# Splitting the tile of log-exponents in a gated-recurrence branch: one tile for keys, one for queries, one more buffer, and a small sum moved from GpSimd to VectorE

## The chip, the cores and the metric

The kernel runs on one core of one Trainium2 chip. The metric is the device time of one launch in microseconds (us). A difference is told against the median of the runs of the kernel before.

Engine names as the profile has them: PE is TensorE's matmul stream, PEld its weight loads, DVE VectorE, ACT ScalarE, POOL GpSimd, SP SyncE. A semaphore is what one engine waits on for another.

## The reference

A trunk of two layers over one sequence of 512 positions with 1024 channels. Each layer has three branches, and the change lies in the first:

```
z = RMSNorm(x) @ W_in            # columns are divided among the branches and gates
A: gated linear recurrence, 4 heads, 128 key and 128 value channels, forward and backward:
     log_f = logaddexp(log lb, log1p(-lb) + logsigmoid(zf));  key = (1 - lb) * sigmoid(-zf)
     state_t = exp(log_f_t) * state_(t-1) + key_t v_t ;  o_t = q_t . state_t   (chunks of 64)
     forward and backward o summed, RMS-normalized per head, times a SiLU gate
B: gated spatial mixing in chunks of 128
C: windowed attention, 8 query heads and 2 key heads of 64 channels, partial rotary, a sink logit
merge: each branch @ W_branch, times a sigmoid gate from xn, summed, @ W_out, added to x
x = x + (relu(RMSNorm(x) @ W_up) ** 2) @ W_down
```

After both layers comes a last RMSNorm. Everything is float32.

## The kernel before, in words

**Products.** Activations lie transposed (channels on the 128 partitions, the 512 positions along the free dimension). Every large product is done with three matmuls of 512 columns (`mm3`, L200 to L202), for which weights and activations are each split into a rounded high part and the low rest. A weight chunk of 512 KB is loaded on SP's queue, its high part is cast on ACT (L195, tile `wh`) and its low part subtracted on DVE (L196, tile `wl`). So all three engines serve the matmuls, beside what the branches themselves ask of ACT and DVE.

**Branch A, one head.** `a_ffb` does the head's two gate projections (matmuls into `f`, brought to the tile `z` on DVE in L693). `a_gates` turns them into a tile `ex` of four rows of 512 exponents: rows 0 and 2 hold the log keys of the forward and the backward direction, rows 1 and 3 the log forget gates that become the exponents of the queries. `a_head` then goes through seven levels L = 1, 2, 4 ... 64. Each level

- exponentiates a half of the query rows into `qt` (ACT, L552), multiplies it with the queries (DVE, L553), exponentiates a half of the key rows into `kt` (ACT, L555),
- does 16 small matmuls (`at`, L539) and puts the result where a mask says (DVE, L543; at L = 1 and L = 64 copies on ACT),
- and adds decays in place to the exponents: two sums of 512 columns on DVE (L580). Each of the two touches a key row and a query row.

At L = 1 there is also the diagonal: one exponential of both key rows (1024 columns, tile `key`, ACT L560), their sum into `dg` on POOL (L562), and 16 more matmuls. After the last level, for each direction the keys are decayed (`kd`, ACT L592), transposed on PE (`kT`, L595), copied (ACT, L597) and multiplied into states (`stp` on PE, L600; `st` on DVE), and the queries are decayed (`qd`, L609 and L610). Then `av` (PE, L623), its norm (`asq` on ACT, L628; `ms` on DVE, L260; `rs` on POOL, L262; `ao` on DVE, L631) and a transposition (`oT`, PE L635).

`qt`, `kt`, `dg`, `kd`, `qd`, `asq` and `ao` take turns in three buffers of the tag "a". `z`, `key` and a work tile of `a_gates` take turns in three buffers of another tag.

**Around it.** While the heads run, PE fills its time with the projections of the next heads (`f`), of branch C (`q`, with rotary on DVE in L867 to L870, L685 and L898), of the gates (`gz`) and of the merge (`yB`, `yC`, `yA`). Branch C's scores `sc` (L914, L915), transposed probabilities `pT` (L943) and products `po` (L948) are mixed in. Transfers of the merge (`mcd`, `th`, `mC`, `mB`) and of the residual (`xr`) are issued by POOL. A turn on PE (`mT`, L1023) sums them up after the last head.

**Who sets the order.** A scheduler with priorities builds the order of each engine's instructions from the program and from its own estimates of time; work of the merge has a low priority and fills. Each engine then runs its list strictly in that order, and waits at an instruction whose input or buffer isn't there. A change of the program therefore also changes which fill work stands between two steps of a head.

Of the kernel before, what the change touches and what calls it, by code (L numbers as in the profile page):

```python
# [10 lines left out]
ALU = mybir.AluOpType  # L11
# [48 lines left out]
def trunk(tc, xT, xt, ws, vec, fnb, bsb, snk, wst, rope, cmask, amask, ident, out):  # L60
# [4 lines left out]
    def pool(**kw):  # L65
# [21 lines left out]
    part = {}  # L87
    BANKS = {"m": 2, "a": 2, "c": 2, "s": 2}
    GROUPS = (("m", "m", "c", "c"), ("a", "a", "s", "s"))
    WR, WB, NZ, NCT, NSM, NQ = 2, 3, 3, 4, 3, 10  # L90

    def nm(s):
        ctr[0] += 1
        return f"{s}_{ctr[0]}"
# [13 lines left out]
        return part["br"].tile([P, 2, S], F32, tag="z2", bufs=NZ, name=nm(name))  # L108

    def SM(tag, w):  # L110
        return pad.tile([P, w], F32, tag="sm_" + tag, bufs=4 if tag == "lb" else NSM, name=nm(tag))

    def CT(name):
        return part["br"].tile([P, 3 * P], F32, tag="ct", bufs=NCT, name=nm(name))
# [384 lines left out]

    def a_gates(l, h, z2, lbs):  # L500

        ex = part["br"].tile([P, 4, S], F32, tag="ex", bufs=1, name=nm("ex"))
        lfo = [ex[:, 3], ex[:, 1]]
        e = Z2("ga")
        nc.scalar.activation(e, z2, AF.Abs)
        nc.scalar.activation(e, e, AF.Exp, scale=-1.0)
        nc.scalar.activation(e, e, AF.Ln, bias=onep_t[:, 0:1])
        if l == 0:
            for d in range(2):
                nc.vector.scalar_tensor_tensor(lfo[d], z2[:, d], 0.0, e[:, d], ALU.min, ALU.subtract)  # L510
                nc.vector.tensor_tensor(ex[:, 2 * d], lfo[d], z2[:, d], ALU.subtract)
        else:
            l1p, llb, dl = lbs
            u = e
            nc.vector.scalar_tensor_tensor(u, z2, 0.0, e, ALU.min, ALU.subtract)
            for d in range(2):
                c = slice(d * 4 + h, d * 4 + h + 1)
                nc.vector.scalar_tensor_tensor(ex[:, 2 * d], u[:, d], l1p[:, c], z2[:, d], ALU.add, ALU.subtract)
# [6 lines left out]
        return ex  # L525

    def a_head(l, h, ex, q, vt):
        H = P // 2
        at = part["br"].tile([P, 4, P], F32, tag="at", bufs=1, name=nm("at"))
        own = part["br"].tile([P, 4, H], F32, tag="own", bufs=1, name=nm("own"))  # L530

        def attn(kk, qq, other=False):

            pt = PT("a", "at")
            for st in range(4):
                for h_ in range(2):
                    k0 = st * P + h_ * H
                    q0 = st * P + (1 - h_ if other else h_) * H
                    nc.tensor.matmul(pt[h_ * H:(h_ + 1) * H, st * H:(st + 1) * H], kk[:, k0:k0 + H], qq[:, q0:q0 + H], start=True, stop=True, skip_group_check=True)  # L539
# [5 lines left out]
        X, R, Y, PP = 0, S, 2 * S, 3 * S  # L545
        for li, L in enumerate(LEVELS):
            nb = 256 // L
            shp = "p (b h i) -> p b h i"
            e_k = ap_of(ex, 0, [[2 * L, nb], [2 * S + L, 2], [1, L]])
            e_q = ap_of(ex, S, [[2 * L, nb], [2 * S + L, 2], [1, L]])  # L550
            qt = T("a", "qt")
            nc.scalar.activation(qt.rearrange(shp, b=nb, h=2), e_q, AF.Exp)  # L552
            nc.vector.tensor_tensor(qt, qt, q, ALU.mult)  # L553
            kt_ = T("a", "kt")
            nc.scalar.activation(kt_.rearrange(shp, b=nb, h=2), e_k, AF.Exp)  # L555
            if L == 1:
                pt = attn(kt_, qt)
                nc.scalar.copy(own, pt)
                key = Z2("key")
                nc.scalar.activation(key, ap_of(ex, 0, [[2 * S, 2], [1, S]]), AF.Exp)  # L560
                dg = T("a", "dg")
                nc.gpsimd.tensor_tensor(dg, key[:, 0], key[:, 1], ALU.add)  # L562
# [13 lines left out]
            d = [[2 * L, nb], [1, L]]  # L576
            z = [[2 * L, nb], [0, L]]
            for o_, ostep, i_, istep in ((X, PP + L - X, PP + 2 * L - 1, -L), (Y + L, R - Y - L, R, L)):
                o_ap = ap_of(ex, o_, [[ostep, 2]] + d)
                nc.vector.tensor_tensor(o_ap, o_ap, ap_of(ex, i_, [[istep, 2]] + z), ALU.add)  # L580

        W3 = 3 * P
        dec = SM("ms", 4)
        nc.scalar.activation(dec[:, 0:2], ap_of(ex, PP + 2 * P - 1, [[P, 2]]), AF.Exp)
        nc.scalar.activation(dec[:, 2:4], ap_of(ex, R + P, [[P, 2]]), AF.Exp)
        sts, qds = [], []
        for dr, (ko, qo) in enumerate(((0, P), (P, 0))):

            kd = T("a", "kd")[:, 0:W3]
            nc.scalar.activation(kd, ex[:, 2 * dr, ko:ko + W3], AF.Exp)  # L592
            pt = PT("a", "kT")
            for i in range(3):
                nc.tensor.transpose(pt[:, i * P:(i + 1) * P], kd[:, i * P:(i + 1) * P], id_t)  # L595
            kT = part["br"].tile([P, W3], F32, tag="kT", bufs=1, name=nm("kT"))
            nc.scalar.copy(kT, pt[:, 0:W3])  # L597
            ps_ = PT("a", "stp")
            for i in range(3):
                nc.tensor.matmul(ps_[:, i * P:(i + 1) * P], kT[:, i * P:(i + 1) * P], vt[ko // P + i][:, h * P:(h + 1) * P], start=True, stop=True)  # L600
# [8 lines left out]
            nc.scalar.activation(qd, ex[:, 3 - 2 * dr, qo:qo + W3], AF.Exp)  # L609
            nc.vector.tensor_tensor(qd, qd, q[:, qo:qo + W3], ALU.mult)  # L610
            sts.append(st_)
            qds.append(qd)

        po = PT("a", "av")
        for tt in range(4):
            c = slice(tt * P, (tt + 1) * P)
            parts = [(at[:, tt], vt[tt][:, h * P:(h + 1) * P])]
            if tt > 0:
                parts.append((qds[0][:, (tt - 1) * P:tt * P], sts[0][:, tt - 1]))
            if tt < 3:  # L620
                parts.append((qds[1][:, c], sts[1][:, tt]))
            for i, (w_, m_) in enumerate(parts):
                nc.tensor.matmul(po[:, c], w_, m_, start=i == 0, stop=i == len(parts) - 1)  # L623
        sq = T("a", "asq")
        ss = SM("ss", 4)
        for tt in range(4):
            c = slice(tt * P, (tt + 1) * P)
            nc.scalar.activation(sq[:, c], po[:, c], AF.Square, accum_out=ss[:, tt:tt + 1])  # L628
        rc = rstd_c(ss, P)
        o = T("a", "ao")  # L630
        nc.vector.tensor_tensor(o.rearrange("p (a b) -> p a b", a=4), po.rearrange("p (a b) -> p a b", a=4), ap_of(rc, 0, [[1, 4], [0, P]]), ALU.mult)  # L631
# [639 lines left out]
```

## Time and profile before

| | |
|---|---|
| median of 3 runs | 1727.49 us (1726.69 to 1728.23) |
| the profiled run | 1725.17 us, its span 1723.3 us |
| mean granted clock of TensorE | 0.993 |
| heads of layer 0 / layer 1 | about 160 to 460 us / 1015 to 1320 us |
| matmuls | 8536 |

The profile covers the span; some 2 us of the run lie around it. Busy time of an engine is the sum of its instructions' durations without overlap. "[2.30 <-DVE qt L553]" behind a row of the timeline says that the engine was idle for 2.30 us before this instruction and that the last thing it waited for was DVE's instruction of line 553 on tile `qt`.

### The profile page before, as it was taken

The page shows a single profiled execution, that of the slowest core. Times are in us where ns is not written, and L with a number is a line of the kernel's source. Part 1 is how long each engine was busy: PE and PEld are TensorE (multiplying, and loading weights), DVE is VectorE, ACT ScalarE, POOL GpSimd, SP SyncE. Part 2 cuts the span into 40 slices and gives each one's busy share as a digit, 9 for nine tenths or more (in the row PEclk, how much of TensorE's full clock was granted, in tenths as well). Part 3 has the DMA queues.
Part 4 walks back from the last instruction along what each step waited for, and adds up shares of the span by engine and source line. Part 5 has one row for each costly group of instructions (what it writes and reads, how often), then busy time and mean ns, then how long its engine had stood idle before and what let it go on. Part 6 is the DMA issues. An engine that isn't in the chain of part 4 may idle for free.

```text
span 1723.3 us, 23007 instructions
## 1 busy us (share of the span) xinstructions
PE 1677.8 (97%) x8536; PEld 1380.8 (80%) x8536; DVE 1288.6 (75%) x2031; ACT 1009.1 (59%) x1691; POOL 150.9 (9%) x215
## 2 busy tenths in 40 slices
PE   6999999999999999999999999999999999999997
PEld 5888877888878888888878887788878788888886
DVE  7996986678465858687889869876875667676867
ACT  6665577677425555454666665877782355545464
POOL 1021210100220000000010202001004100000001
PEclk9999999999999999999999999999999999999999
DMA  8243221222465232332332332222315453232311
GB/s 317 76 147 109 75 95 63 98 87 86 141 230 191 86 123 95 114 103 95 132 123 98 135 103 86 92 69 97 104 56 220 178 182 106 98 110 86 123 62 49
DMA packets 58143, 199.84 MB, mean 116 GB/s; under 512 B 7888, under 2 KB 8144, under 8 KB 58032
## 3 DMA queue, kind: packets, MB, share of 16 engines
q1 hardware_dynamic: 44496, 154.46, 26.2%
q0 software_dynamic: 13248, 43.40, 6.7%
q8 instruction: 67, 1.10, 0.3%
q10 hardware_dynamic: 288, 0.52, 0.1%
q14 instruction: 44, 0.36, 0.1%
HBM read 177.38 MB, written 20.97 MB: 115 GB/s over the span
## 4 chain that ended last, share of the span: by engine, by line
PE 81%; DVE 8%; ACT 5%; issue 4%; DMA 2%; POOL 1%; SPq 0%; POOLq 0%; DVEq 0%; ACTq 0%
PE up L200 7%; PE up L201 7%; PE up L202 7%; PE dA L406 3%; PE dA L407 3%; PE dA L408 3%; PE po L948 2%; PE wo L243 2%; PE wo L242 2%; PE dC L407 2%; PE dC L406 2%; PE dC L408 2%; PE wo L244 2%; PE gz L202 1%; PE gz L201 1%
## 5 line engine op out<-in xcount | busy, mean ns | idle before, releaser
L195 ACT CAST wh<-wq 128x1024 fp32r<-128x1024 f32 x196 | 206.2, 1052 | 211.6 <-PE dA L407 50.8
L196 DVE TENSOR_TENSOR wl<-wr,wh 128x1024 fp32r<-128x1024 f32 x171 | 208.9, 1222 | 154.5 <-ACT wh L195 153.8
L195 ACT CAST wh<-wr 128x1024 fp32r<-128x1024 f32 x171 | 179.2, 1048 | 230.9 <-PE up L201 88.3
L196 DVE TENSOR_TENSOR wl<-wq,wh 128x1024 fp32r<-128x1024 f32 x196 | 239.2, 1222 | 87.5 <-ACT wh L195 86.2
L201 PE MATMUL up<-xl,wh 128*128 128x512 f32 x512 | 199.3, 390 | 0.0
L202 PE MATMUL up<-xh,wl 128*128 128x512 f32 x512 | 199.3, 390 | 0.0
L200 PE MATMUL up<-xh,wh 128*128 128x512 f32 x512 | 198.8, 390 | 0.0
L202 PEld LDWEIGHTS up<-xh,wl 128*128 128x128 f32 x512 | 96.2, 188 | 20.1
L200 PEld LDWEIGHTS up<-xh,wh 128*128 128x128 f32 x512 | 96.2, 188 | 19.8
L201 PEld LDWEIGHTS up<-xl,wh 128*128 128x128 f32 x512 | 96.2, 188 | 19.7
L406 PE MATMUL dA<-wh,sh 128*128 128x512 f32 x256 | 99.8, 390 | 0.0
L407 PE MATMUL dA<-wh,sh 128*128 128x512 f32 x256 | 99.7, 390 | 0.0
L408 PE MATMUL dA<-wl,sh 128*128 128x512 f32 x256 | 92.7, 390 | 0.0
L580 DVE TENSOR_TENSOR ex<-ex 128x512 f32<-128x512 f32 x112 | 74.9, 685 | 4.8 <-ACT kt L555 4.5
L552 ACT ACTIVATE qt<-ex 128x512 f32<-128x512 f32 x56 | 37.8, 675 | 50.1 <-DVE ex L580 39.0
L262 POOL TENSOR_TENSOR rs<-ms,mhalf_t 128x4 f32<-128x4 f32 (+2 forms) x15 | 18.5, 1232 | 497.6 <-DVE ms L260 493.4
L408 PEld LDWEIGHTS dA<-wl,sh 128*128 128x128 f32 x256 | 48.1, 188 | 10.0
L406 PEld LDWEIGHTS dA<-wh,sh 128*128 128x128 f32 x256 | 48.1, 188 | 9.9
L407 PEld LDWEIGHTS dA<-wh,sh 128*128 128x128 f32 x256 | 48.1, 188 | 9.9
L200 PE MATMUL gz<-xh,wh 128*128 128x512 f32 x128 | 51.6, 403 | 0.0
L202 PE MATMUL gz<-xh,wl 128*128 128x512 f32 x128 | 51.4, 402 | 0.0
L201 PE MATMUL gz<-xl,wh 128*128 128x512 f32 x128 | 51.1, 399 | 0.0
(405 smaller groups left out, 4352.2 us busy)
## 6 DMA issues: line engine op xcount, KB each, us to landing
wr<-in_ws_dram SPq DMA_DIRECT2D x171, 512.0 KB, 3.3
wq<-in_ws_dram SPq DMA_DIRECT2D x112, 512.0 KB, 4.2
thd<-zt POOLq DMA_DIRECT2D x32, 256.0 KB, 2.6
th<-thd POOLq DMA_DIRECT2D x32, 256.0 KB, 4.4
mgd<-mg POOLq DMA_DIRECT2D x16, 256.0 KB, 2.4
mcd<-th POOLq DMA_DIRECT2D x16, 256.0 KB, 2.6
mC<-mcd POOLq DMA_DIRECT2D x16, 256.0 KB, 6.2
mB<-mgd POOLq DMA_DIRECT2D x16, 256.0 KB, 5.9
```

The costliest lines, as they stand in the source:

```text
L195: nc.scalar.copy(hi, raw)
L196: nc.vector.tensor_tensor(lo, raw, hi.bitcast(F32), ALU.subtract)
L200: nc.tensor.matmul(pt, whi, xhi, start=first, stop=False)
L201: nc.tensor.matmul(pt, whi, xlo, start=False, stop=False)
L202: nc.tensor.matmul(pt, wlo, xhi, start=False, stop=last)
L242: nc.tensor.matmul(pts[t], xh, hi[:, c], start=k == 0, stop=False)
L243: nc.tensor.matmul(pts[t], xl, hi[:, c], start=False, stop=False)
L406: nc.tensor.matmul(pt, xh[:, t], hi[:, c], start=start and k == 0, stop=False, skip_group_check=True)
L407: nc.tensor.matmul(pt, xl[:, t], hi[:, c], start=False, stop=False, skip_group_check=True)
L408: nc.tensor.matmul(pt, xh[:, t], lo[:, c], start=False, stop=k == 3, skip_group_check=True)
L552: nc.scalar.activation(qt.rearrange(shp, b=nb, h=2), e_q, AF.Exp)
L580: nc.vector.tensor_tensor(o_ap, o_ap, ap_of(ex, i_, [[istep, 2]] + z), ALU.add)
```

## The change

The tile `ex` becomes two: `kx` with the two key rows and `qx` with the two query rows. Each level exponentiates keys first and queries second, and its two sums are now one for the keys (`kx` plus decays from `qx`, L579) and one for the queries (`qx` in place, L580). The diagonal uses two exponentials of 512 columns (`dg` and `kb`, ACT L560 and L561) and a sum on DVE (L562) in place of one exponential of 1024 columns and a sum on POOL. The tag "a" has four buffers, `qd` two of its own; the tag of `z` has two in place of three, a small tag of branch C (`gsc`) too. Lines behind the levels move up by two (L592 becomes L590 and so on).

```
-             "q": 2, "a": 3, "g": 2, "ch": 10,
+             "q": 2, "a": 4, "g": 2, "ch": 10,
-    WR, WB, NZ, NCT, NSM, NQ = 2, 3, 3, 4, 3, 10
+    WR, WB, NZ, NCT, NSM, NQ = 2, 3, 2, 4, 3, 10
-        ... bufs=4 if tag == "lb" else NSM ...
+        ... bufs={"lb": 4, "gsc": 2}.get(tag, NSM) ...
...
-        ex = part["br"].tile([P, 4, S], F32, tag="ex", bufs=1, name=nm("ex"))
+        kx = part["br"].tile([P, 2, S], F32, tag="kx", bufs=1, name=nm("kx"))
+        qx = part["br"].tile([P, 2, S], F32, tag="qx", bufs=1, name=nm("qx"))
...
-            e_k = ap_of(ex, 0, [[2 * L, nb], [2 * S + L, 2], [1, L]])
-            e_q = ap_of(ex, S, [[2 * L, nb], [2 * S + L, 2], [1, L]])
+            half = [[2 * L, nb], [S + L, 2], [1, L]]
+            kt_ = T("a", "kt")
+            nc.scalar.activation(kt_.rearrange(shp, b=nb, h=2), ap_of(kx, 0, half), AF.Exp)
             qt = T("a", "qt")
-            nc.scalar.activation(qt.rearrange(shp, b=nb, h=2), e_q, AF.Exp)
+            nc.scalar.activation(qt.rearrange(shp, b=nb, h=2), ap_of(qx, 0, half), AF.Exp)
             nc.vector.tensor_tensor(qt, qt, q, ALU.mult)
-            kt_ = T("a", "kt")
-            nc.scalar.activation(kt_.rearrange(shp, b=nb, h=2), e_k, AF.Exp)
             if L == 1:
...
-                key = Z2("key")
-                nc.scalar.activation(key, ap_of(ex, 0, [[2 * S, 2], [1, S]]), AF.Exp)
-                dg = T("a", "dg")
-                nc.gpsimd.tensor_tensor(dg, key[:, 0], key[:, 1], ALU.add)
+                dg, kb = T("a", "dg"), T("a", "kb")
+                nc.scalar.activation(dg, kx[:, 0], AF.Exp)
+                nc.scalar.activation(kb, kx[:, 1], AF.Exp)
+                nc.vector.tensor_tensor(dg, dg, kb, ALU.add)
...
-            for o_, ostep, i_, istep in ((X, PP + L - X, PP + 2 * L - 1, -L), (Y + L, R - Y - L, R, L)):
-                o_ap = ap_of(ex, o_, [[ostep, 2]] + d)
-                nc.vector.tensor_tensor(o_ap, o_ap, ap_of(ex, i_, [[istep, 2]] + z), ALU.add)
+            k_ap, q_ap = ap_of(kx, 0, d), ap_of(qx, 0, d)
+            nc.vector.tensor_tensor(k_ap, k_ap, ap_of(qx, S + 2 * L - 1, [[1 - S - 2 * L, 2]] + z), ALU.add)
+            nc.vector.tensor_tensor(q_ap, q_ap, ap_of(qx, L, [[S - 1, 2]] + z), ALU.add)
...
-            qd = T("a", "qd")[:, 0:W3]
+            qd = part["br"].tile([P, W3], F32, tag="qd", bufs=2, name=nm("qd"))
```

**How the lists move.** First, ACT in layer 0 at the start of head 0 (levels 1 and 2); numbers behind a name tell tiles of one name apart. Before:

```order
L552 ACTIVATE qt_1384<-ex_1340 128x512
L555 ACTIVATE kt_1387<-ex_1340 128x512
L560 ACTIVATE key_1399<-ex_1340 128x1024
L250 CAST yh_1737<-bu_325 128x512
L195 CAST wh_1846<-wr_1844 128x1024
L250 CAST yh_1741<-bu_327 128x512
L558 COPY own_1383<-at_1389 128x256
L552 ACTIVATE qt_1415<-ex_1340 128x512
L555 ACTIVATE kt_1418<-ex_1340 128x512
```

ACT at the same place after the change:

```order
L552 ACTIVATE kt_1385<-kx_1340 128x512
L554 ACTIVATE qt_1387<-qx_1341 128x512
L560 ACTIVATE dg_1400<-kx_1340 128x512
L561 ACTIVATE kb_1401<-kx_1340 128x512
L250 CAST yh_1739<-bu_325 128x512
L195 CAST wh_1848<-wr_1846 128x1024
L552 ACTIVATE kt_1417<-kx_1340 128x512
L250 CAST yh_1743<-bu_327 128x512
L558 COPY own_1384<-at_1390 128x256
L554 ACTIVATE qt_1419<-qx_1341 128x512
```

The key exponential of level 2 has moved ahead of a cast and of the copy of level 1; the query exponential stays behind them.

Second, PE in layer 0 at the end of head 0's levels: `at_1505` is level 64, `kT_1525` the first transposition of decayed keys, `f_456` a projection for a later head. Before:

```order
L539 MATMUL at_1505<-qt_1500,kt_1503 64x64 x8
L200 MATMUL f_456_2154<-xh_163,wh_2150 128x512
L201 MATMUL f_456_2154<-xl_164,wh_2150 128x512
L202 MATMUL f_456_2154<-xh_163,wl_2151 128x512
L200 MATMUL f_456_2154<-xh_167,wh_2150 128x512
L201 MATMUL f_456_2154<-xl_168,wh_2150 128x512
L202 MATMUL f_456_2154<-xh_167,wl_2151 128x512
L200 MATMUL f_456_2154<-xh_171,wh_2150 128x512
L201 MATMUL f_456_2154<-xl_172,wh_2150 128x512
L202 MATMUL f_456_2154<-xh_171,wl_2151 128x512
L200 MATMUL f_456_2154<-xh_175,wh_2150 128x512
L595 MATMUL kT_1525<-id_t,kd_1523 128x128 x3
```

PE at the same place after:

```order
L200 MATMUL f_453_2124<-xh_163,wh_2120 128x512
L541 MATMUL at_1507<-qt_1504,kt_1502 64x64 x8
L593 MATMUL kT_1527<-id_t,kd_1525 128x128 x3
L201 MATMUL f_453_2124<-xl_164,wh_2120 128x512
L202 MATMUL f_453_2124<-xh_163,wl_2121 128x512
```

Ten projection matmuls stood between level 64 and the transposition; now none does. Between the diagonal's matmuls and level 64, PE's list now has 119 matmuls of 512 columns where it had 142.

Third, PE in layer 1 at the end of the last head: the end of `av`, then `oT`, with the merge's `yC` and `yA`. Before (19 matmuls of the merge stand between the last `av` and `oT`; the last of them are shown):

```order
L242 MATMUL yC_11700<-wh_11734,yh_11606 128x512
L243 MATMUL yC_11700<-wh_11734,yl_11607 128x512
L244 MATMUL yC_11700<-wl_11735,yh_11606 128x512
L242 MATMUL yC_11701<-wh_11734,yh_11606 128x512
L243 MATMUL yC_11701<-wh_11734,yl_11607 128x512
L244 MATMUL yC_11701<-wl_11735,yh_11606 128x512
L635 MATMUL oT_11287<-id_t,ao_11285 128x128 x4
```

PE at the same place after:

```order
L621 MATMUL av_11280<-vt_8024,at_11100 128x128
L621 MATMUL av_11280<-st_11254,qd_11258 128x128
L941 MATMUL pT_10545<-id_t,sc_10350 128x128 x2
L946 MATMUL po_10549<-pT_10540,cvt_9417 128x256 x2
L633 MATMUL oT_11303<-id_t,ao_11301 128x128 x4
L242 MATMUL yC_11634<-wh_11670,yh_11622 128x512
```

Now four small matmuls of branch C stand between the last `av` and `oT`, and the merge's matmuls follow behind it.

More of the change, by code (lines that the diff above doesn't have):

```diff
@@ L110, in SM @@
     def SM(tag, w):
-        return pad.tile([P, w], F32, tag="sm_" + tag, bufs=4 if tag == "lb" else NSM, name=nm(tag))
+        return pad.tile([P, w], F32, tag="sm_" + tag, bufs={"lb": 4, "gsc": 2}.get(tag, NSM), name=nm(tag))
     def CT(name):
@@ L500, in a_gates @@
     def a_gates(l, h, z2, lbs):
[L502 to L503 removed]
+        kx = part["br"].tile([P, 2, S], F32, tag="kx", bufs=1, name=nm("kx"))
+        qx = part["br"].tile([P, 2, S], F32, tag="qx", bufs=1, name=nm("qx"))
+        lfo = [qx[:, 1], qx[:, 0]]
         e = Z2("ga")
@@ L510, in a_gates @@
                 nc.vector.scalar_tensor_tensor(lfo[d], z2[:, d], 0.0, e[:, d], ALU.min, ALU.subtract)
-                nc.vector.tensor_tensor(ex[:, 2 * d], lfo[d], z2[:, d], ALU.subtract)
+                nc.vector.tensor_tensor(kx[:, d], lfo[d], z2[:, d], ALU.subtract)
         else:
@@ L517, in a_gates @@
                 c = slice(d * 4 + h, d * 4 + h + 1)
-                nc.vector.scalar_tensor_tensor(ex[:, 2 * d], u[:, d], l1p[:, c], z2[:, d], ALU.add, ALU.subtract)
+                nc.vector.scalar_tensor_tensor(kx[:, d], u[:, d], l1p[:, c], z2[:, d], ALU.add, ALU.subtract)
                 nc.scalar.activation(z2[:, d], u[:, d], AF.Abs, bias=dl[:, c])
@@ L524, in a_gates, with a_head @@
                 nc.vector.tensor_tensor(lfo[d], u[:, d], z2[:, d], ALU.add)
-        return ex
-    def a_head(l, h, ex, q, vt):
+        return kx, qx
+    def a_head(l, h, kqx, q, vt):
+        kx, qx = kqx
         H = P // 2
@@ L591, in a_head @@
             kd = T("a", "kd")[:, 0:W3]
-            nc.scalar.activation(kd, ex[:, 2 * dr, ko:ko + W3], AF.Exp)
+            nc.scalar.activation(kd, kx[:, dr, ko:ko + W3], AF.Exp)
             pt = PT("a", "kT")
```

9 lines of the change are left out of this document (4 added, 5 removed).

## The prediction

> **What bounds the kernel now.** I read the profile's busy shares first, then the stretches in which the change acts, then what PE waits for there, and last the single rows that price each moved step.
>
> ```profile
> PE 1677.8 (97%) x8536; PEld 1380.8 (80%) x8536; DVE 1288.6 (75%) x2031; ACT 1009.1 (59%) x1691; POOL 150.9 (9%) x215
> PE 81%; DVE 8%; ACT 5%; issue 4%; DMA 2%; POOL 1%; SPq 0%; POOLq 0%; DVEq 0%; ACTq 0%
> ```
>
> PE is busy 1677.8 of 1723.3 us, and the chain that ended last lies on it for 81%. The change leaves the matmuls as they are, so it can win only PE's idle time, 45.5 us in all, and a lower granted clock. The windows show where these lie (columns: stretch and length, busy time of PE, weight loads, DVE, ACT and POOL, granted clock, DMA share, GB/s):
>
> ```profile
> 160.00:460.00 300.00, 291.62 (x1829) 239.31 (x1828) 226.32 (x466) 198.72 (x411) 32.10 (x37) 0.99 0.26 89
> 460.00:545.00 85.00, 80.72 (x375) 65.46 (x374) 47.16 (x66) 28.03 (x45) 20.18 (x37) 0.98 0.57 211
> 1015.00:1320.00 305.00, 296.97 (x1852) 243.53 (x1851) 235.16 (x462) 216.68 (x427) 35.72 (x45) 0.99 0.27 91
> 180.00:200.00 20.00, 20.00 (x141) 15.98 (x140) 19.87 (x31) 11.21 (x17) 4.22 (x4) 1.00 0.24 79
> 1055.00:1075.00 20.00, 20.00 (x128) 15.89 (x128) 19.97 (x32) 8.79 (x14) 4.55 (x4) 1.00 0.28 92
> 260.00:280.00 20.00, 16.11 (x104) 12.78 (x103) 11.95 (x34) 17.31 (x36) 0.56 (x1) 0.83 0.20 67
> 1075.00:1095.00 20.00, 16.53 (x95) 13.12 (x95) 18.57 (x36) 12.74 (x26) 0.99 (x2) 0.91 0.23 79
> 1280.00:1300.00 20.00, 16.26 (x135) 12.71 (x130) 14.27 (x31) 15.85 (x40) 1.17 (x3) 1.00 0.10 31
> 480.00:500.00 20.00, 16.79 (x72) 12.65 (x72) 13.28 (x21) 4.48 (x6) 7.84 (x15) 0.91 0.93 365
> ```
>
> The heads of layer 0 (160 to 460) leave PE 8.4 us idle, those of layer 1 (1015 to 1320) 8.0, the merge's transfers behind layer 0 4.3. Nearly half of the heads' share sits in three stretches: 3.9 us in 260 to 280, 3.5 in 1075 to 1095, 3.7 in 1280 to 1300. The first two also had a granted clock of 0.83 and 0.91, up to 0.17 x 20 = 3.4 and 0.09 x 20 = 1.8 us. So at most 16.4 us of idle time and some 5 of clock are there to win in the heads. In head 0 (180 to 200 and 1055 to 1075) PE is never idle and DVE is full, 19.87 and 19.97 of 20 us: there fill work hides every wait of branch A, and DVE is what a head can be late on.
>
> What PE waits for in the two stretches of heads (line waited for, total us, times, longest), and, last, what ACT waits for in the whole span:
>
> ```profile
> PE at L539 <- DVE qt L553: 2.3, 1, 2.3
> PE kT L595 <- ACT kd L592: 2.0, 1, 2.0
> PE stp L600 <- ACT kT L597: 1.6, 2, 1.3
> PE q L200 <- DVE z L693: 3.5, 1, 3.5
> PE po L948 <- ACT pT L944: 1.9, 2, 1.5
> ACT qt L552 <- DVE ex L580: 39.0, 17, 5.0
> ```
>
> ACT stood 39.0 us before the next level's exponential, because both sums had to be through. PE waited for a level itself only once, for 2.3 us. The wait that the split shortens is thus large on ACT and almost invisible on PE.
>
> **The change part by part.**
>
> *The split tiles.* There are as many sums as before, of the same size.
>
> ```profile
> L580 DVE TENSOR_TENSOR ex<-ex 128x512 f32<-128x512 f32 x112 | 74.9, 685 | 4.8 <-ACT kt L555 4.5
> L560 ACT ACTIVATE key<-ex x8: 1045/1055/1065, 179.4 to 1237.5; 128x1024 f32<-128x1024 f32 x8
> L552 ACT ACTIVATE qt<-ex x56: 613/633/892, 177.8 to 1287.7; 128x512 f32<-128x512 f32 x56
> L562 POOL TENSOR_TENSOR dg<-key x8: 1272/1284/1379, 180.5 to 1262.1; 128x512 f32<-128x512 f32 x8
> ```
>
> 112 sums of 685 ns stay 112; none is saved. The key sum needs only the key exponential of its level, the query sum only the query exponential, so the two chains overlap. Its worth is a shorter level, and that moves the list on PE: level 64 of head 0 stands 23 matmuls nearer to the diagonal. How long one takes shows in the starts of rows in the timeline:
>
> ```profile
> 225.69 0.40 PE L202 MATMUL f<-xh,wl 128*128 128x512 f32 x1
> 225.92 0.40 PE L200 MATMUL f<-xh,wh 128*128 128x512 f32 x1
> 228.29 0.55 PE L595 MATMUL kT<-id_t,kd 128*128 128x128 f32 x3 [1.97 <-ACT kd L592]
> 218.41 0.68 DVE L553 TENSOR_TENSOR qt<-qt,q 128x512 f32<-128x512 f32 x1
> 223.12 0.69 PE L539 MATMUL at<-qt,kt 128*64 128x64 f32 x16
> ```
>
> 23 x 0.23 = 5.2 us earlier. The last query product was done at 219.1, four us ahead of its matmuls at 223.12, where the key exponential was the later one; on DVE's list that product moves up by about four instructions, some 2.8 us by their 0.6 to 1.2 us each. So PE asks at about 217.9 for what comes at about 216.3: it fits, with 1.6 us to spare. Behind it the transposition loses the ten matmuls that covered it, but `kd` now follows the query exponential at once, so I let most of the 1.97 us wait go and give back up to a microsecond at tighter levels: -0.7 us in layer 0. In layer 1 I take 1.0 off the 3.5 us wait for `z`: -1.0. Bounds: -2.0 and -3.5 if these waits vanish, +5.2 (layer 0) if DVE's list doesn't come forward at all.
>
> *The stretch 260 to 280.* Head 1's levels wait here between table loads of ACT, 3.9 us idle and up to 3.4 of clock. Levels 1 and 2 stand 9.3 us apart on PE's new list, in place of 5.2, others stand closer. I take -2.5; bounds -6.8 and +0.5.
>
> *The diagonal.* ACT: 16 x 0.633 for 8 x 1.055, +1.7 us; ACT is idle 41% of the span and nothing queued behind it is late in head 0. DVE gets 8 more sums, POOL loses 8. What one costs DVE and what POOL's cost it:
>
> ```profile
> 180.07 0.68 DVE L828 SCALAR_TENSOR_TENSOR bu<-yb,bu 128x512 f32<-128x512 f32 x1
> 180.67 1.78 DVE L553 TENSOR_TENSOR qt<-qt,q 128x512 f32<-128x512 f32 x1
> 180.53 1.38 POOL L562 TENSOR_TENSOR dg<-key 128x512 f32<-128x512 f32 x1 [15.75 <-ACT key L560]
> ```
>
> Sums start 0.60 us apart, so DVE gains 8 x 0.6 = 4.8 us of work. But the product at 180.67 took 1.78 us in place of 0.68, while POOL's sum ran. With such excesses on DVE adding up to an estimated 2.8 us over all 8, DVE is left with about +2 us over the program, and in head 0 with half a microsecond less. In the Trainium skill, "SBUF — State Buffer", section "SBUF: two separate sides", the port pair that VectorE and GpSimd share is an exclusive lock, and a VectorE operation with two SBUF inputs and a GpSimd operation that reads SBUF block each other for a whole instruction. By that rule all of POOL's 8 x 1.28 = 10.3 us could have stood in DVE's way, and DVE would come out 5.5 us lighter; the trace agrees on the mechanism, while only part of that time met such an operation. I set 0 for the diagonal (bounds -2 and +2): DVE's work reaches PE only where DVE is late.
>
> *The end of the last head.* Now `oT` follows `av` after four small matmuls, where 19 of the merge stood. The chain between them, in layer 1:
>
> ```profile
> 1308.40 0.39 PE L623 MATMUL av<-st,qd 128*128 128x128 f32 x2
> 1308.82 0.28 ACT L628 ACTIVATE asq<-av 128x128 f32<-128x128 f32 x1 [1.19 <-PE av L623]
> 1311.32 0.69 DVE L631 TENSOR_TENSOR ao<-av,rs 128x512 f32<-128x512 f32 x1 [1.16 <-POOL rs L262]
> ```
>
> From the last `av` to the end of `ao` are 1312.01 - 1308.40 = 3.6 us; four small matmuls cover 0.7 of it, so PE waits about 3 us, a wait that before had 19 x 0.23 = 4.4 us of cover. In layer 1 the end of the head had 3.7 us idle in 1280 to 1300 and some more behind it; by the list the steps of the head that caused them stand earlier and looser, and I take -4.7 for them: net -1.7. In layer 0 less was idle there (the 1.3 us of `stp` is of this kind): +3 - 1.1 = +1.9. Bounds: 0 and -4.7, and +3 for each layer.
>
> *The transfers behind layer 0.* 480 to 500 left 3.2 us idle at a clock of 0.91. POOL's list ran into this:
>
> ```profile
> 471.06 2.16 POOL L957 DMA_DIRECT2D th<-thd  x4 [7.15 <-DMA mcd<-th]
> ```
>
> The loads of `th` wait for the stores of `mcd`; four loads of the residual stood amid the last stores. On the new list three of them stand ahead of all but the first of these stores, and the last merge matmul and first `mT` come 5 us closer. I take -2 us; bounds -5 and +1.
>
> *The buffers.* One more "a" buffer and `qd` of its own take away waits of later exponentials; two in place of three for `z` can delay a projection's eviction. The only such wait on PE is the 3.5 us counted above; for all the rest -0.5 (-2 to +3).
>
> Sum: -0.7 - 1.0 - 2.5 - 1.7 + 1.9 - 2 - 0.5 = -6.5, rounded to -6 of the profiled run's 1725.2 us: 1719. The median of the runs lies 2.3 above it, so I give 1727.5 - 6 = 1721.5 us.
>
> **The rivals.**
>
> *Given back (about 1727).* The gains above are all in single stretches, and the wait at `oT` is new. For it speaks that two single waits of 3 to 4 us came with clocks of 0.83 and 0.91, which cost 1.8 to 3.4 us more; against it that 3.7 us in several pieces (1280 to 1300) left the clock at 1.00. Two `oT` waits with a dip each, 2 x 2.6 = 5.2, eat nearly all: 1726.7. The Trainium skill, "TensorE: Matmul & The Clock Gate", Part 1 ("The HAM clock gate"), states that the clock halves after an idle window of about 3.4 us and returns after one such window busy, the windows running freely. By that rule a wait of 3 us alone wouldn't trip it, and the forecast would stand; the rows of 0.83 and 0.91 agree with it, for both hold about 3.5 us of idle time or more.
>
> *Slower: PE asks head 0 sooner than DVE delivers (about 1733.5).* Level 64 stands 5.2 us sooner in layer 0 and 4.8 in layer 1 on PE, while DVE is busy 19.87 and 19.97 of 20 us and its work doesn't shrink. If the query products don't come forward, PE waits up to 10 us, less the 2 of the `kd` wait and with the 2 of other gains: +6. It decides if the last query product of head 0 starts later than about 217.2 us, 1.2 sooner than now. For it: full DVE; against it: the shorter list ahead of this product, and the 4 us that it has to spare now.
>
> *All waits go (about 1707).* If loosened levels let fill work cover the heads fully, 16.4 us and 5 of clock vanish: some -20. Against it stands that most of these waits are for `z`, `pT` and `po`, which the change leaves alone.
>
> *The change does nothing* (within the first rival): PE waited for a level once.
>
> **How the numbers follow.** A measurement of this kernel can tell about 0.2%, 3.5 us, from no change. Forecast 0.47, its own range 1712 to 1724; given back 0.22; DVE late 0.26, more than its spare time alone would give, since the whole list moved and any other tight product would do the same; all waits gone 0.05. Faster by over 0.2% is 0.47 + 0.05 = 0.52, within it 0.22, slower 0.26. The range runs from 1711, the sum's parts near their better bounds, to 1735, which takes in the second case and over half of the third; what it leaves out is the last case and the far end of the third.
>
> **What would show it.** Right: in the heads PE idles about 5 us less over both layers, the ACT wait for the sums falls from 39 us to under 20, `kT` in head 0 waits under 0.5 us, `oT` at the end of each layer's last head waits about 3 us, 260 to 280 has a clock above 0.9. Wrong: level 64's matmuls waiting for `qt` in head 0, or several microseconds of idle time in 180 to 220 or 1055 to 1075, would make it slower; a clock below 0.9 around the last `oT` would give the gain back; and an unchanged idle total in the heads would mean that the split reaches only ACT.

## The result, and the profile after

The changed kernel took 1731.24 us (median of 8 runs, 1729.72 to 1732.54) against 1726.7 (8 runs): a ratio of 1.0026, with a 95% interval of 1.0015 to 1.0037. It is slower by 4.5 us. The profiled run took 1732.54 us, its span 1730.7, with a mean clock of 0.992. Runs of one kernel differ by some microseconds, and with the granted clock: of 31 runs of the kernel before on one chip, those at 0.994 took 1723.1 to 1724.5 us, those at 0.988 and 0.989 1728.0 to 1728.7.

The page's busy shares, then the four stretches of the heads and the merges (columns as in the prediction):

```profile
PE 1684.4 (97%) x8536; PEld 1380.8 (80%) x8536; DVE 1291.1 (75%) x2039; ACT 1008.8 (58%) x1699; POOL 137.6 (8%) x207
160.00:460.00 300.00, 291.08 (x1833) 238.30 (x1833) 227.64 (x470) 200.00 (x416) 28.68 (x40) 1.00 0.28 93
460.00:545.00 85.00, 81.77 (x378) 66.89 (x377) 47.14 (x66) 28.39 (x45) 17.37 (x31) 0.96 0.56 200
1015.00:1320.00 305.00, 297.64 (x1856) 243.63 (x1856) 236.57 (x467) 217.44 (x432) 29.69 (x41) 0.99 0.28 93
```

Two things stand out. PE's idle time in the heads is the same: 8.9 + 7.4 = 16.3 us, where it was 8.4 + 8.0. And PE's busy time has grown by 6.7 us, from 1677.8 to 1684.4, with the same 8536 matmuls. The span grew by 7.4 us at nearly the same clock (0.993 and 0.992), so most of that growth is not waiting; something makes matmuls themselves longer. What PE waits for in the heads of layer 0 and of layer 1, and in the merges behind them (one row of each):

```profile
PE po L946 <- ACT pT L942: 2.8, 2, 1.5
PE pT L941 <- ACT yc L948: 2.7, 2, 1.6
PE q L200 <- DVE z L691: 0.9, 1, 0.9
PE oT L633 <- DVE ao L629: 0.7, 1, 0.7
...
PE at L541 <- DVE qt L555: 2.3, 1, 2.3
PE po L946 <- ACT pT L942: 1.8, 2, 1.3
...
PE mT L1021 <- DVE mC L1042: 2.6, 1, 2.6
...
PE mT L1021 <- DVE mC L1042: 2.7, 1, 2.7
```

The wait for `kd` at `kT` (2.0) and the long one for `z` (3.5) have gone, as has the one of 2.3 us for `qt` at 260 to 280. The wait of 1.6 us for `yc` at `pT` there has stayed, and one of 1.5 for `pT` at `po` has come beside it. New are a wait for `qt` in head 0 of layer 1 and one at `mT` behind each layer.

**Where PE's busy time grew.** The MLP has no line of the change in it. Rows of PE's timeline there, 18 matmul starts apart; first before, then after:

```profile
605.38 0.39 PE L406 MATMUL dA<-wh,sh 128*128 128x512 f32 x1
...
609.46 0.39 PE L406 MATMUL dA<-wh,sh 128*128 128x512 f32 x1
```

```profile
605.49 0.39 PE L406 MATMUL dA<-wh,sh 128*128 128x512 f32 x1
...
609.61 0.39 PE L406 MATMUL dA<-wh,sh 128*128 128x512 f32 x1
```

4.08 / 18 = 227 ns before, 4.12 / 18 = 229 ns after. The same engine's `up` products are as fast as before. The groups of these tiles by line (min/median/max ns), before and after:

```profile
L406 PE MATMUL dA<-wh,sh x256: 388/390/476, 583.6 to 1713.7; 128*128 128x512 f32 x128
L200 PE MATMUL up<-xh,wh x512: 388/390/397, 538.3 to 1675.6; 128*128 128x512 f32 x171
L200 PE MATMUL yB<-yh,wh x64: 387/390/477, 245.6 to 1232.4; 128*128 128x512 f32 x64
```

```profile
L406 PE MATMUL dA<-wh,sh x256: 388/392/478, 583.5 to 1721.1; 128*128 128x512 f32 x128
L200 PE MATMUL up<-xh,wh x512: 389/389/397, 538.2 to 1682.6; 128*128 128x512 f32 x171
L200 PE MATMUL yB<-yh,wh x64: 388/394/481, 243.6 to 1244.6; 128*128 128x512 f32 x64
```

What `dA` and `yB` share, and `up` does not, is an operand (the stationary `sh`, the moving `yh`) in a part of SBUF that the change has moved. The one line that gives `gsc` two buffers in place of three makes the pool of small tiles 64 bytes shorter. Nearly every large tile allocated after it (`yh`, `sh`, `xs`, `mgh` and all of the branches' tiles) starts 64 bytes lower, at 448 or 960 modulo 1024, where it was 512 or 0. `xh`, `wh` and `wl` lie ahead of that pool and stay at multiples of 512. Matching each 512-column matmul of the trace with the addresses of the built program gives, for directly following pairs:

| operand in the displaced part | pairs after | before: mean spacing | after |
|---|---|---|---|
| none | 3841 | 227.4 ns | 227.6 |
| the stationary one | 2135 | 227.2 | 229.3 |
| the moving one (`yB`) | 159 | 228.8 | 233.2 |

Worked out: 2135 x 2.16 ns + 159 x 4.4 ns + 3841 x 0.22 ns = 4.6 + 0.7 + 0.8 = 6.1 us, most of the 6.7 us of busy time. The profile doesn't show addresses, but sorting its matmuls by tile name alone shows the same: `dA` products started 226.8 ns apart before and 229.0 after, `up` 226.7 in both, and `yA`, whose stationary operand lies ahead of the pool, 226.9 and 227.2.

### The profile page after: what moved, and what is told of

Its sections match the earlier page's. It is cut to its first block, busy times and chain, and to the rows that moved or that the text cites. A ratio compares the mean times of both kernels' runs of the same rounds, so it can differ in the third digit from the quotient of the medians.

```text
span 1730.7 us, 23011 instructions
## 1 busy us (share of the span) xinstructions
PE 1684.4 (97%) x8536; PEld 1380.8 (80%) x8536; DVE 1291.1 (75%) x2039; ACT 1008.8 (58%) x1699; POOL 137.6 (8%) x207
## 4 chain that ended last, share of the span: by engine, by line
PE 81%; ACT 6%; DVE 5%; issue 4%; DMA 2%; POOL 1%; SPq 0%; POOLq 0%; DVEq 0%; ACTq 0%
PE up L201 7%; PE up L202 7%; PE up L200 7%; PE dA L407 3%; PE dA L406 3%; PE dA L408 3%; PE wo L242 2%; PE wo L243 2%; PE gA L406 2%; PE wo L244 2%; PE po L946 2%; PE dC L407 2%; PE dC L408 2%; PE dC L406 2%; PE gA L408 2%
## 5 line engine op out<-in xcount | busy, mean ns | idle before, releaser
L552 ACT ACTIVATE kt<-kx 128x512 f32<-128x512 f32 x56 | 37.8, 675 | 26.0 <-DVE kx L579 16.5
L243 PE MATMUL wo<-wh,mgl 128*128 128x512 f32 x128 | 51.6, 403 | 0.0
L554 ACT ACTIVATE qt<-qx 128x512 f32<-128x512 f32 x56 | 37.6, 671 | 23.4 <-DVE qx L580 22.0
```

The lines of the kernel that those rows point to most:

```text
L243: nc.tensor.matmul(pts[t], xl, hi[:, c], start=False, stop=False)
L552: nc.scalar.activation(kt_.rearrange(shp, b=nb, h=2), ap_of(kx, 0, half), AF.Exp)
L554: nc.scalar.activation(qt.rearrange(shp, b=nb, h=2), ap_of(qx, 0, half), AF.Exp)
```

## The experiments

Three theories were to be told apart. *Placement*: the 64 bytes cost some 6 us, and the reordering is worth little. *Order*: the new lists cost the time, by the waits at `mT`, `oT` and `qt`. *A disturbed run*: the slower matmuls belong to the one profiled run. All ratios are to the kernel before on the same chip, with 95% intervals.

**The same lists at other places.** Buffers of small tiles of which fewer are needed than made, or that never decide the order, shift all the rest. In the kernel before, `gsc` with 2, 5 or 7 buffers moves it by -64, +128 or +256 bytes; in the changed kernel, fewer buffers of small tiles move it by -128 or -512 in all. Each engine's list stays word for word that of its original (the -512 kernel also makes `pad_t`, a tile of 16 columns, one of 8).

```
before, -64:    bufs={"lb": 4, "gsc": 2}.get(tag, NSM)      # +128: "gsc": 5    +256: "gsc": 7
after, -128:    bufs={"lb": 4, "gsc": 2, "r2": 2, "s4": 2}.get(tag, NSM)
after, -512:    bufs={"lb": 4, "gsc": 1, "r2": 2, "s4": 1, "ss8": 1, "ss": 2, "rs": 2, "ms": 2, "bn": 2, "mv": 2, "lr": 2}
                pad_t = pad.tile([P, 8], F32, name="pad_t")
```

The changed kernel again:

> The changed kernel once more, on the chip of the next three. Placement theory: in the profile after, matmuls of 512 columns whose stationary or moving operand starts 64 bytes off a multiple of 128 bytes start 229 to 233 ns apart, others 227.5; that is a property of the build and comes back: the same tiles slow, 1731 us, +4 to +5 against before. Rival, a disturbed run: the spacing is 227 everywhere this time and the time nearer to 1726.

The kernel before, 64 bytes lower:

> The kernel before with two in place of three buffers for one small tile of which only two are ever made. Every engine's list stays word for word as before; only the tiles allocated behind it move down by 64 bytes (1024 modulo 2048 becomes 960). Placement theory: +5.5 to +6.5 us (about 1732), spacing 229 to 233 ns in the products that read these tiles (dA, dB, dC, yB, wo, gA), 227 in up. Order theory (the loss comes from the new order and its new waits at oT and mT): no change, within 2 us of before.

The kernel before, 128 bytes higher:

> The kernel before with five in place of three of these buffers: lists as before, the tiles behind move up by 128 bytes. Placement theory with 128 bytes as the grain: no change, within 1 us of before. With a coarser grain (256 or 512 bytes): +4 to +6 us. Order theory: no change.

The changed kernel, 128 bytes lower in all:

> The changed kernel with two more small tiles of two buffers in place of three, lists word for word those of the changed kernel, the tiles behind moved down by another 64 bytes, so 128 in all. Placement theory with a grain of 128: 6 us less than the changed kernel, 1725, that is about 1 to 2 us below before. Placement with a coarser grain: 1730 to 1732. Order theory: 1731 as the changed kernel.

The changed kernel, 512 bytes lower in all:

> The changed kernel with fewer buffers of small tiles, so that the tiles behind them lie 512 bytes lower than in the kernel before, at 512 modulo 1024 in place of 960; the lists are word for word those of the changed kernel. Placement theory with a grain of 512: 5 to 7 us less than the changed kernel, 1724 to 1726, all matmuls 227 ns apart; what is left against before is the worth of the new order, -1.5 to +1 us. If placement isn't it: 1731.

The kernel before, 256 bytes higher:

> The kernel before, lists word for word, tiles behind the small ones 256 bytes higher. If the cost grows with the distance from the nearest multiple of 512 (64 bytes: 2 ns on the stationary operand, 128 bytes: 5 ns): about 10 ns, 1745 to 1752. If 256 is a grain of its own: 1726. If any offset of 128 or more costs the same: 1739.

Measured:

| lists of | displaced by | spacing, stationary operand displaced | us (runs) | ratio to before |
|---|---|---|---|---|
| before | 0 | 227.2 ns | 1725.8 to 1726.7 (in each comparison) | 1 |
| before | +256 | 227.1 | 1726.57 (10) | 1.0004 (0.9995 to 1.0013) |
| before | -64 | 229.3 | 1732.46 (5) | 1.0037 (1.0023 to 1.0051) |
| before | +128 | 232.5 | 1738.99 (5) | 1.0081 (1.0067 to 1.0096) |
| after | -512 | 227.1 | 1724.8 (11) | 0.9991 (0.9982 to 1.0000) |
| after | -64 (as it is, again) | 229.3 | 1731.08 (7) | 1.0026 (1.0015 to 1.0037) |
| after | -128 | 232.7 | 1738.15 (5) | 1.0072 (1.0059 to 1.0084) |

Both families fall into the same steps: nothing at a multiple of 256 bytes, +6 to +7 us at 64 off, +13 at 128 off. The grain is thus 256 bytes, not the 128 that two of the expectations took as the first case (and their other case, a coarser grain, was priced at 4 to 6 us, not at 13), and 256 off costs nothing where an offset that grew would have cost 20. In the three kernels where the stationary operand lies at a multiple of 256, 64 off and 128 off, the same group reads so (before, +256; before, -64; before, +128):

```profile
L406 PE MATMUL dA<-wh,sh x256: 388/389/477, 583.0 to 1714.0; 128*128 128x512 f32 x128
```

```profile
L406 PEld LDWEIGHTS dA<-wh,sh x256: 187/188/190, 581.7 to 1716.5; 128*128 128x128 f32 x128
L406 PE MATMUL dA<-wh,sh x256: 388/392/479, 581.9 to 1716.7; 128*128 128x512 f32 x128
```

```profile
L406 PEld LDWEIGHTS dA<-wh,sh x256: 187/188/192, 585.5 to 1726.8; 128*128 128x128 f32 x128
L406 PE MATMUL dA<-wh,sh x256: 389/393/479, 585.7 to 1727.0; 128*128 128x512 f32 x128
605.16 0.39 PE L406 MATMUL dC<-wh,sh 128*128 128x512 f32 x1
...
609.33 0.40 PE L406 MATMUL dA<-wh,sh 128*128 128x512 f32 x1
```

The last two rows are again 18 starts apart: 4.17 / 18 = 232 ns. The weight loads themselves (PEld) stay at 188 ns. The disturbed run is out: the changed kernel's second profile has the same spacing (its PE busy time was 1681.4 us at a clock of 0.995, so some 3 us of busy time go with the clock of a run; the spacing doesn't). The order theory is out as the cause of the loss: with its lists untouched and its tiles at multiples of 256, the changed kernel is 1.1 us below before (by the interval, 0 to 3.1). So the loss divides into about +6.3 us of placement (1731.1 - 1724.8; the same 64 bytes cost the kernel before 6.6) and -1.1 us for everything that the change was described as. The -512 kernel also has fewer buffers of small tiles, which might cost it a wait.

**The parts at undisturbed places.** Why was the order worth -1 and not the -6 of the forecast? Each part alone, and together, with all large tiles at multiples of 256.

The split alone (three buffers of tag "a", diagonal as before):

```
kernel before, with kx and qx, key exponential first, sums as in the change, and
+                nc.scalar.activation(key, kx, AF.Exp)       # still summed on POOL
```

> The kernel before with the split tiles alone (key exponential first, one sum for keys and one for queries), diagonal still summed on POOL, buffers as before, and all tiles at the places of before. If the split's shorter levels win PE time: 1720 to 1724. If new waits take it back, or the level's length was hidden: 1725 to 1728.

Buffers alone (`"a": 4`, `NZ` 2), and split with these buffers:

> The kernel before with four buffers of tag a and two of z's, nothing else changed, all tiles read by matmuls at multiples of 256 bytes. If the fourth buffer is of use only together with the split (in before ACT waits for the sums, not for buffers): 1725 to 1728. If the buffer alone is the gain: 1720 to 1723. If two z buffers hurt by themselves: 1729 or more.

> Split tiles with four buffers of tag a and two of z's, the diagonal still one exponential of 1024 and a sum on POOL; places as before. With the split alone ACT waited 17.0 us for PE to free buffers (13.7 at qt, 3.3 at kt); if that was what cost it 3.5 us, this is back at 1721 to 1725. If it is the order of the list by chance: 1726 to 1731.

The diagonal's sum alone:

```
-                nc.gpsimd.tensor_tensor(dg, key[:, 0], key[:, 1], ALU.add)
+                nc.vector.tensor_tensor(dg, key[:, 0], key[:, 1], ALU.add)
```

> The kernel before with the diagonal's sum on VectorE in place of POOL, nothing else; places as before. By the prediction's own price (8 x 0.6 us on DVE less the holds by POOL, little of it on PE): 1725 to 1727. If POOL's sum held up head 0, which DVE bounds: 1722 to 1724.

The diagonal with the split, and with the buffers (each is the two edits above together):

> Split tiles and the diagonal's sum on VectorE, three buffers of tag a and three of z's as before, places as before. If the parts add up (split +3.5, diagonal -5.4): 1723 to 1725. If the split is harmful only beside POOL's sum: 1719 to 1721. If the order of the list decides and the parts say nothing of each other: anything from 1718 to 1732.

> Four buffers of tag a, two of z's and the diagonal's sum on VectorE, without the split; places as before. If the parts add up (buffers -1.8, diagonal -5.4): 1718 to 1720, the fastest so far. If the order decides: 1720 to 1730.

The whole change without `qd`'s own buffers, and the whole change with one buffer of tag "g":

```
-            qd = part["br"].tile([P, W3], F32, tag="qd", bufs=2, name=nm("qd"))
+            qd = T("a", "qd")[:, 0:W3]                       # and "gsc" three buffers again
```

> The whole change without qd's own buffers (qd in the four of tag a), so that three buffers of the small tile fit and nothing is displaced. Placement theory: 1724 to 1727, all matmuls 227 ns apart, whatever the order. Order theory: about 1731.

> The whole change, qd's own buffers too, with one in place of two buffers of tag g so that three buffers of the small tile fit and nothing is displaced by less than 256 bytes. Placement theory: 1720 to 1727, matmuls 227 ns apart. Placement refuted: 1731.

| kernel | us (runs) | ratio to before |
|---|---|---|
| diagonal | 1720.43 (5) | 0.9968 (0.9956 to 0.9981) |
| whole change, `qd` in tag "a" | 1721.2 (9) | 0.9972 (0.9962 to 0.9982) |
| buffers + diagonal | 1722.38 (6) | 0.9973 (0.9962 to 0.9985) |
| buffers | 1724.05 (11) | 0.9991 (0.9982 to 1.0000) |
| whole change (-512) | 1724.8 (11) | 0.9991 (0.9982 to 1.0000) |
| split | 1729.43 (11) | 1.0016 (1.0007 to 1.0025) |
| split + diagonal | 1729.61 (12) | 1.0018 (1.0008 to 1.0028) |
| split + buffers | 1729.88 (11) | 1.0022 (1.0013 to 1.0031) |
| whole change, one "g" buffer | 1731.35 (5) | 1.0032 (1.0019 to 1.0045) |

The split, meant to shorten each level, made the kernel slower where it stood alone. What ACT waits for in that kernel, as to `qt` and `kt`:

```profile
ACT qt L554 <- PE at L541: 13.7, 11, 3.8
ACT kt L552 <- DVE kx L579: 5.6, 5, 1.7
ACT kt L552 <- PE at L541: 3.3, 1, 3.3
```

The sums hold ACT for 5.6 us in place of 39.0; the three buffers now hold it for 17.0, until PE has read them. More buffers were expected to bring the time back to 1721 to 1725; that kernel took 1729.88, so this expectation failed and the buffers are not the whole cause. On PE the split alone loses at the ends of both layers (the timeline of layer 0, and the end of layer 1 as a stretch):

```profile
455.54 0.39 PE L621 MATMUL av<-st,qd 128*128 128x128 f32 x2
459.27 0.66 PE L633 MATMUL oT<-id_t,ao 128*128 128x128 f32 x4 [3.34 <-DVE ao L629]
...
1300.00:1320.00 20.00, 15.52 (x77) 12.66 (x76) 10.31 (x18) 5.01 (x13) 6.03 (x11) 0.86 0.36 124
```

Here `oT` stands directly behind `av`, with nothing in between: 3.3 us of waiting, as the prediction priced that chain, and a clock of 0.86 around the one in layer 1. The same wait stands in split + diagonal (3.4 in each layer). In split + buffers PE waits only 0.7 us at each `oT`, and that kernel is as slow, so this wait alone is not the cause either.

The diagonal's sum on VectorE, priced at nothing, gave the largest gain. The stretch 240 to 300 of before and of that kernel:

```profile
240.00:300.00 60.00, 54.84 (x349) 44.83 (x349) 44.80 (x117) 42.86 (x96) 5.09 (x7) 0.94 0.21 75
```

```profile
240.00:300.00 60.00, 59.18 (x397) 48.38 (x396) 45.81 (x123) 46.09 (x108) 3.80 (x6) 1.00 0.25 84
```

5.2 us of idle time became 0.8, and the clock went from 0.94 to 1.00: the group of waits in head 1 at 260 to 280 is gone. But the list changed there too: PE's two levels stand elsewhere among the fill work. So no run separates a cheaper sum from a luckier list.

The parts don't add up. The buffers alone, 1724.05, fell between the two cases of their expectation; buffers + diagonal, 1722.4, were slower than the sum of both (1718 to 1720). Split + diagonal would be +3.5 - 5.4 = -1.9 us and was about +3; the split beside both others went along with -4.7. Whole change with `qd` in tag "a" and whole change at -512 lie 3.6 us apart; they differ in `qd`'s buffers, but also in those of small tiles. Three results lay outside every case of their expectation: split alone (1729.4), diagonal alone (1720.4) and `qd` in tag "a" (1721.2). The one-"g" kernel also takes a buffer away, and its lists are others than the changed kernel's, so that its loss may come from either; its displaced part is at multiples of 512 and its matmuls are 227 ns apart (`dA` 389 ns). What it has in its place is more waiting (49.8 us of PE idle time against 44.9 in the -512 kernel) and a lower clock (0.990 against 0.993). So 227 ns comes with the places, whatever the time; and the run refutes the expectation that good places alone keep a kernel under 1727.

## Why the prediction was wrong, step by step

The prediction failed at two steps. It had no term for the places of the operands (+6.3 us). And it priced only the waits that it had looked at, most of them about rightly; on the other stretches it put nothing, and new waits came there. PE's idle time by stretch, in the two profiled runs (in us; "clock" is the granted one):

| stretch | forecast | idle before | idle after | clock |
|---|---|---|---|---|
| 160 to 260 (head 0, layer 0) | -0.7 | 3.4 | 2.1 | 1.00 in both |
| 260 to 280 | -2.5, clock included | 3.9 | 3.1 | 0.83, then 1.00 |
| 280 to 430 | 0 | 0 | 1.0 | 1.00 in both |
| 430 to 460 (end of the last head) | +1.9 | 1.1 | 2.7 | 1.00 in both |
| 460 to 545 (merge) | -2 | 4.3 | 3.2 | 0.98, then 0.96 |
| 1055 to 1095 (head 0, layer 1) | -1.0 | 3.5 | 2.9 | a dip to 0.91 in both |
| 1095 to 1280 | 0 | 0.8 | 1.8 | 1.00 in both |
| 1280 to 1320 (end of the last head) | -1.7 | 3.7 | 2.7 | 1.00 in both |
| 1320 to 1400 (merge) | 0 | 1.3 | 3.6 | 1.00, then 0.98 |
| sum | -6.0 | 22.0 | 23.1 | 0.993 and 0.992 over the run |

The three stretches with a forecast of nothing took 4.3 us. The 1.1 us of the sum and the 6.7 of busy time make up the growth of the span (7.4) within half a microsecond. In the -512 kernel the same stretches sum to 20.9, 1.1 below before, as its time says. (The stretches lie at the same times in both runs, so that a wait near an edge can fall to its neighbour.)

- **What fails first: the places of the operands.** The smaller `gsc` is named nowhere in the sum; it is at most part of "all the rest" in "The buffers", priced at -0.5 us (-2 to +3), as waits alone. It measured +6.3 us, not as a wait but as slower reading by PE in stages that the change doesn't touch. No view of before could have shown that price, as all large tiles there lie at multiples of 512; but the premise "The change leaves the matmuls as they are, so it can win only PE's idle time" should have been checked against where the operands lie, too. With this term the forecast sum is -6.5 + 6.3, about 0; the rest of the miss is the table's.
- **The split, mechanism.** The prediction expected ACT's wait for the sums to fall from 39 to under 20 us. It became two waits of about the same total:

```profile
L552 ACT ACTIVATE kt<-kx 128x512 f32<-128x512 f32 x56 | 37.8, 675 | 26.0 <-DVE kx L579 16.5
L554 ACT ACTIVATE qt<-qx 128x512 f32<-128x512 f32 x56 | 37.6, 671 | 23.4 <-DVE qx L580 22.0
```

  16.5 + 22.0 = 38.5 us. With three buffers, in the split alone, the sums held ACT for only 5.6 us, so the fall that was forecast came there, and the time still rose. The named sign "an unchanged idle total in the heads would mean that the split reaches only ACT" is what came: 16.4 us before, 16.3 after, 15.3 in the -512 kernel, where 5 less was the sign of being right.
- **Head 0.** The `kT` wait went, as forecast. In layer 1 the wait for `z` fell from 3.5 to 0.6, but now a level waited 2.3 us for `qt`: the head and the mechanism of the second rival (PE asks sooner than DVE delivers), though not at level 64, and at less than a quarter of the 10 us that it allowed for. PE's timeline and the stretch:

```profile
1068.95 1.12 PE L541 MATMUL at<-qt,kt 128*64 128x64 f32 x16 [2.30 <-DVE qt L555]
...
1055.00:1075.00 20.00, 17.70 (x111) 13.64 (x110) 19.97 (x31) 7.03 (x12) 4.69 (x3) 0.91 0.24 80
```

  DVE is full, as it was, and PE, which had no idle time there, now has 2.3 us and a clock of 0.91. The time came out on that rival's side (slower) for another reason.
- **260 to 280.** Clock above 0.9: right (1.00). Idle time fell only from 3.9 to 3.1 us; the clock came back whole, which is up to 3.4 us more. But in this run the dips moved rather than went: 480 to 500 fell from 0.91 to 0.83, 1320 to 1400 from 1.00 to 0.98, and the mean clock of the run stayed. (Also, the three stretches named in the prediction hold 11.1 of the heads' 16.4 us, two thirds and not "nearly half".)

```profile
260.00:280.00 20.00, 16.87 (x131) 13.06 (x130) 15.86 (x38) 18.92 (x39) 0.55 (x1) 1.00 0.23 74
480.00:500.00 20.00, 16.85 (x70) 13.17 (x69) 12.85 (x19) 5.60 (x7) 6.56 (x12) 0.83 0.88 344
```

- **The end of the last head.** A wait of about 3 us at `oT` was forecast. PE waited 1.3 us at `po`, one of the four small matmuls, and 0.7 at `oT`:

```profile
1297.28 1.13 PE L946 MATMUL po<-pT,cvt 128*128 128x256 f32 x4 [1.28 <-ACT pT L942]
1299.14 0.66 PE L633 MATMUL oT<-id_t,ao 128*128 128x128 f32 x4 [0.72 <-DVE ao L629]
```

  Together 2.0 of the 3, and the net changes, -1.0 and +1.6 us, are near the -1.7 and +1.9 of the forecast. The first rival's clock dip did not come there in this run; in the -512 kernel, with the same lists and the same 2.0 us of idle time, it did (second row):

```profile
1280.00:1300.00 20.00, 18.00 (x105) 15.17 (x104) 7.38 (x18) 11.28 (x34) 1.04 (x1) 1.00 0.15 53
1280.00:1300.00 20.00, 18.00 (x95) 15.16 (x94) 11.03 (x20) 8.38 (x23) 4.11 (x7) 0.91 0.16 49
```

- **The transfers.** -2 us was taken behind layer 0 because residual loads moved ahead; about half of it came (4.3 to 3.2 us). Behind layer 1, where the prediction put nothing, idle time rose by 2.3 us; the stretch 1320 to 1400 before and after:

```profile
1320.00:1400.00 80.00, 78.71 (x378) 65.06 (x377) 46.12 (x64) 27.88 (x45) 15.69 (x29) 1.00 0.62 235
```

```profile
1320.00:1400.00 80.00, 76.44 (x357) 61.99 (x356) 46.05 (x65) 27.68 (x44) 16.01 (x29) 0.98 0.58 208
```

  The new wait in both layers is `mT` for the sum `mC`, 2.6 and 2.7 us, where the waits of before at this place were 0.4 us in all. It looks like a load that came late, and the stores did land later in the changed kernel (5.5 us against 2.6 in the middle, the loads 7.3 against 6.2). The rows behind layer 1 show another cause; DVE before, then DVE and one row of POOL after:

```profile
1328.02 1.22 DVE L196 TENSOR_TENSOR wl<-wr,wh 128x1024 fp32r<-128x1024 f32 x1
1329.15 1.29 DVE L1044 TENSOR_TENSOR mC<-mC,th 128x512 f32<-128x512 f32 x2
```

```profile
1331.27 1.89 DVE L1042 TENSOR_TENSOR mC<-mC,th 128x512 f32<-128x512 f32 x3
1338.02 1.23 DVE L196 TENSOR_TENSOR wl<-wr,wh 128x1024 fp32r<-128x1024 f32 x1 [4.86 <-ACT wh L195]
1339.16 0.68 DVE L1042 TENSOR_TENSOR mC<-mC,th 128x512 f32<-128x512 f32 x1
1333.08 0.54 POOL L1036 DMA_DIRECT2D mC<-mcd  x1 [0.45 <-DMA mC<-mcd]
```

  After, three of the four sums run, and the fourth stands on DVE's list behind the low part `wl` of a weight chunk, for which DVE waits 4.9 us until ACT has made `wh` (4.7 us in layer 0). The fourth sum's own load was through six microseconds before: POOL's next load, which had to wait for it, was issued at 1333.1. Before, no `wl` that has to wait stands there. The other kernels agree: in every merge where the fourth sum stands behind a `wl` that waits (2.8 to 6.1 us), the longest wait of `mT` for `mC` is 0.5 to 3.8 us; in the others it is at most 0.3. Buffers + diagonal has such a `wl`, and waits 2.7 and 1.7 us, although its stores land in 3.0 us. Why `wh` itself is late differs: in layer 0 ACT waited for PE's `yA`, in layer 1 for the load of the weights. The prediction read the lists of PE and POOL here and not DVE's, and counted it as a gain that the last merge matmul and the first `mT` come 5 us closer.
- **The clock.** 1055 to 1075 of the changed kernel shows 0.91 with one wait of 2.3 us and no other idle time. 260 to 280 of before shows 0.83 with waits of 2.3 and 1.6 us, which the prediction counted as a single wait of 3 to 4. And 2.0 us of idle time at 1280 to 1300 came once with 1.00 and once with 0.91. The prediction took from the Trainium skill, "TensorE: Matmul & The Clock Gate", "Part 1: The HAM clock gate", that the clock halves after an idle window of about 3.4 us, so that a wait of 3 us alone wouldn't trip it. The measured rows differ from that rule: at 1055 to 1075 a wait of 2.3 us was enough.
- **What held.** PE bounds the kernel, DVE bounds head 0, matmul and sum counts are unchanged, and at undisturbed places the change is a gain, if a small one: about 1 us (0 to 3.1), not 6. The forecasts for the ends of the last heads were near, and so was that for head 0 of layer 1, there by luck: two errors in the waits for `z` and `qt` cancel.

## What to carry to other kernels

When a change alters the size of any tile, look where all tiles behind it now start: here 64 bytes less in a pool of tiny tiles cost about 6 us where the rest of the change was worth about 1, in stages that it never touched, and the sign was a matmul row that got 2 ns longer with its neighbours unchanged. To separate such an effect, displace tiles in both kernels with the lists untouched. Where an engine waits for a sum, look at what stands ahead of that sum on its own engine's list before blaming its load. A forecast built from single waits of a reordered list is worth little below a few microseconds: parts of this change measured -5.4 to +3.5 us alone and didn't add up, and the fastest version found is a single line, the diagonal's sum on VectorE, 1720.43 us, a ratio of 0.9968 (0.9956 to 0.9981) to before.

## What the runs showed of the hardware

The address at which an operand of a matmul starts sets its pace. With 128 x 512 float32r matmuls back to back, a stationary operand at a multiple of 256 bytes gave 227 ns a matmul, 64 bytes below a multiple 229.3 ns, 128 bytes off 232.5 ns; a moving operand 64 below or 128 off gave 233 and 232, against 228.8 in the kernel before and up to 230.0 in changed kernels at multiples of 256. Why this is so, and what other offsets do, no run here tells; 32 bytes and 64 above a multiple weren't tried.

The granted clock dipped in stretches whose longest single wait of PE was 2.3 us, and the same 2.0 us of idle time came with and without a dip.
